# A hybrid layer's single-core kernel: slack in a planned order, rotation tables made once, splits and squares moved between engines

## The chip, the core and the metric

One core of one Trainium2 chip runs the whole layer. The metric is the device time of one execution in microseconds. The five engines are PE (TensorE, matmuls), DVE (VectorE), ACT (ScalarE), POOL (GpSimd) and SP (SyncE, which issues most transfers).

## What is computed

A decoder layer for 2048 tokens of width 1024. One projection feeds latent attention (4 heads), a gated delta rule (4 heads, chunked) and attention over 256 memory tokens; the three are gated, projected and added to x. The reference, cut to what matters:

```python
h = rms_norm(x, norm_in[l])
c_q, c_kv, k_rope, gdn_qkv, gdn_a, gdn_b, mem_q, gate = split_cols(h @ w_in[l], IN_SPLITS)
q = (rms_norm(c_q, q_a_norm[l]) @ w_q_b[l])          # 4 heads of 128 + 64
q_rope = apply_rope(q_rope, cos, sin); k_rope = apply_rope(k_rope, cos, sin)
kv = (rms_norm(c_kv, kv_a_norm[l]) @ w_kv_b[l])
o_mla = causal_mla(q_nope, q_rope, k_nope, k_rope, v_mla)
qkv = silu(causal_depthwise_conv(gdn_qkv, gdn_conv[l]))
gq, gk = l2_normalize(gq), l2_normalize(gk)
o_gdn = rms_norm(gated_delta_rule_chunked(gq, gk, gv, g, beta), gdn_norm[l])
o_mem = memory_attention(mem_q, mk, mv)              # mk, mv from rms_norm(mem) @ w_mem_kv
mixed = concatenate([o_mla, o_gdn, o_mem]) * silu(gate)
x = rms_norm(x + mixed @ w_out[l], norm_final)
```

The delta rule solves a triangular system for each chunk and then runs over the chunks in order: `v_new = u - w @ state`, an output from the state and `v_new`, and `state = state * decay + k.T @ v_new`. The reference's chunk is 64 tokens; the kernel takes steps of 128.

## The kernel before

**Tiles and stages.** The sequence is worked in two halves of 1024 tokens, each in two blocks of 512. Matrices lie with features in the 128 partitions. A product in full precision is made of three fast ones: both sides are split into a high part and a rest (`hh`, `hl` of the normed input; `wh`, `wl` of a weight tile `wr`; `bwh`, `bwl` of a weight tile `bw`), so a group of projection matmuls in the trace reads hh,wh / hl,wh / hh,wl. The high part is a cast on ACT, the rest a subtraction on DVE or GpSimd. Matmul results of the projection are named `ip`.

**The opening.** x is loaded transposed; `prepare` splits it for a block and sums its squares into `acc` over eight tiles (squares on ACT, adds on GpSimd or DVE). `channel_rms` reduces that to the inverse norm of each token (tiles xss, nt, rc), `dg` is a diagonal matrix of it, and PE spreads it over the partitions (`rb`), from where ACT copies it to `rms`. `abt` is the first result scaled by it.

**The delta rule.** For every half and head, `delta_head` is a coroutine. It takes the norms of q and k (`sums`, `norms`, `nt`), loads rows that scale them (`fr`) and a decay row (`gr`) for each block, builds `kq` and its products `kk`, lets GpSimd solve the 32x32 diagonal blocks in 62 small operations (`pr`, `X`; input `lt`, output `tsys`), doubles the inverse on PE (`inv`, `mid`) and then runs eight scan steps. A step is: PE `pa` from the state; DVE `r`; PE; ACT `vn`; PE; DVE the new state (`st` and `st_odd` in turn); PE the output. The small tables of decays are the tiles `tks` and, turned by PE through `pc`, `cols`. Convolution blocks (`conv`) write `raw`, whose first three columns are the history `hist` of the block before, and make `y` of it.

**What sets the order.** Nobody writes the order out. A planner in the kernel's Python code keeps a clock for each engine (`T`), adds a modelled cost to it for every instruction, and walks through the projection units; after every three matmuls `pump` looks through the coroutines in the background. A coroutine that says `yield d` is resumed when the planner's PE clock has passed the modelled end of its last step (`step_end`) by d nanoseconds. So a `yield` sets how much other PE work comes between two dependent steps. Every engine then runs its own instructions in exactly that order, and waits where an operand is not there. `lesser` gives the subtraction of a split to GpSimd when GpSimd's clock, and a time called `solving`, are no later than PE's clock plus some slack, and else to DVE. `dma` puts a transfer on SP's queue in the order of its modelled times.

**Rotation tables.** `trig_tables` makes sine and cosine of all positions in two passes of 1024 positions, on 128 partitions in which the 32 frequencies stand four times; products on GpSimd, sines on ACT; the result goes to memory. `key_rope` and the rotation of q load `cs` and `sn` from there.

## Time and profile before

| | us |
|---|---|
| median of 3 runs (1838.02 to 1842.04) | 1840.38 |
| the profiled execution's own time | 1840.0 |
| its span in the trace | 1838.2 |
| PE busy | 1745.6 (95%) |
| DVE busy | 1200.7 (65%) |
| ACT busy | 737.7 (40%) |
| GpSimd busy | 546.9 (30%) |

The mean granted clock of PE is 0.98. The shares are averages over stages: the opening to about 60 us, projections with convolutions to about 170, projections beside solves and scans to about 1000, the hand-over to attention to about 1200, attention and the output projection to the end. A wait in brackets in a timeline is the idle time ahead of an instruction and what ended it.

### The profile page before, as it was taken

How to read it: one execution, taken by the hardware profiler on the slowest of the kernel's cores; microseconds unless marked ns; L12 is line 12 of the kernel's file. 1: busy time of each engine (PE TensorE's matmuls, PEld its weight loads, DVE VectorE, ACT ScalarE, POOL GpSimd, SP SyncE). 2: the span in 40 equal slices, each digit the busy share in tenths (PEclk: the TensorE clock that was granted, in tenths of full speed). 3: DMA queues.
4: the chain of work that ended last, by engine and by line, in shares of the span. 5: the costliest groups of instructions: out<-in, count | busy, mean ns of one | idle time of the engine just before them, and what ended most of it. 6: DMA issues, size and time to landing. Idle time of an engine off the chain costs nothing. (4 is left out here: it accounts for less than half of the span.)

```text
span 1838.2 us, 28677 instructions
## 1 busy us (share of the span) xinstructions
PE 1745.6 (95%) x9780; PEld 1466.7 (80%) x9780; DVE 1200.7 (65%) x2710; ACT 737.7 (40%) x1798; POOL 546.9 (30%) x918
## 2 busy tenths in 40 slices
PE   6898999999989999999998799999999999999998
PEld 5676778787777788888887687889999989878886
DVE  8878796567776777646667363677776778345443
ACT  6354243234343445324444322455555556322121
POOL 6534716341251224443112635001111002412120
PEclk8899999899999999999999999999999999999999
DMA  5444457434646544564566368435252526566551
GB/s 199 154 135 152 149 179 213 132 97 153 199 127 236 166 149 127 176 213 137 171 202 185 99 195 268 139 107 184 67 175 79 155 90 214 165 190 198 176 160 53
DMA packets 226355, 292.51 MB, mean 159 GB/s; under 512 B 30464, under 2 KB 130816, under 8 KB 226208
## 3 DMA queue, kind: packets, MB, share of 16 engines
q1 hardware_dynamic: 219168, 274.94, 47.7%
q0 software_dynamic: 7040, 15.74, 3.0%
q8 instruction: 77, 1.26, 0.3%
q14 instruction: 70, 0.57, 0.1%
HBM read 197.53 MB, written 93.06 MB: 158 GB/s over the span
## 5 line engine op out<-in xcount | busy, mean ns | idle before, releaser
L258 PE MATMUL ip<-hh,wh 128*128 128x512 f32 x1088 | 459.8, 423 | 22.9 <-ACT hh L258 8.4
L258 PE MATMUL ip<-hh,wl 128*128 128x512 f32 x1088 | 434.7, 400 | 5.6 <-DVE wl L258 3.0
L258 PE MATMUL ip<-hl,wh 128*128 128x512 f32 x1088 | 432.4, 397 | 0.2
L258 PEld LDWEIGHTS ip<-hh,wh 128*128 128x128 f32 x1088 | 209.2, 192 | 58.9 <-ACT hh L258 8.4
L258 PEld LDWEIGHTS ip<-hh,wl 128*128 128x128 f32 x1088 | 208.2, 191 | 51.8 <-DVE wl L258 3.8
L258 PEld LDWEIGHTS ip<-hl,wh 128*128 128x128 f32 x1088 | 209.3, 192 | 35.3 <-DVE hl L258 1.1
L258 POOL TENSOR_TENSOR wl<-wr,wh 128x512 fp32r<-128x512 f32 x72 | 98.5, 1368 | 397.5 <-ACT wh L258 374.9
L258 ACT CAST wh<-wr 128x512 fp32r<-128x512 f32 x146 | 90.2, 618 | 144.5 <-PE ip L258 103.8
L258 DVE TENSOR_TENSOR tl<-pt,th 128x512 fp32r<-128x512 f32 (+2 forms) x208 | 119.8, 585 | 28.3 <-ACT th L258 25.9
L258 PE MATMUL sc<-kn,qn 128*128 128x512 f32 (+2 forms) x480 | 134.6, 381 | 0.0
L258 PE MATMUL av<-th,vn 128*128 128x256 f32 x576 | 131.5, 288 | 0.8 <-ACT th L258 0.8
L258 PE MATMUL op<-wop,mh 128*128 128x512 f32 x416 | 130.5, 394 | 0.0
L258 DVE SCALAR_TENSOR_TENSOR y<-raw,gdn_conv,y 128x512 f32<-128x512 f32 x144 | 121.9, 854 | 7.6 <-ACT y L258 6.6
L258 ACT CAST th<-pt 128x512 fp32r<-128x512 f32 (+2 forms) x163 | 82.4, 513 | 102.6 <-PE pt L258 94.1
L258 POOL TENSOR_TENSOR pr<-X,lt 128x60 f32<-128x60 f32 (+24 forms) x248 | 97.8, 394 | 55.7 <-DMA lt<-lsys 37.0
L293 POOL DMA_DIRECT2D mix<-mo x64 | 34.7, 543 | 238.6 <-ACT mo L258 162.2
L258 PEld LDWEIGHTS av<-th,vn 128*128 128x128 f32 x576 | 98.8, 189 | 6.2 <-ACT th L258 2.6
L258 POOL TENSOR_TENSOR X<-X,pr 128x60 f32<-128x60 f32 (+24 forms) x248 | 95.9, 387 | 19.3
L258 PE MATMUL sc<-kr,qr 128*128 128x512 f32 (+2 forms) x320 | 96.7, 381 | 0.0
L258 POOL TENSOR_TENSOR og<-og,orow 128x512 f32<-128x512 f32 x28 | 41.1, 1490 | 170.7 <-DMA orow<-ri 142.9
L258 PEld LDWEIGHTS op<-wop,mh 128*128 128x128 f32 x416 | 77.4, 188 | 17.3
L258 ACT ACTIVATE s<-s,m 128x768 f32<-128x768 f32 (+13 forms) x71 | 79.0, 1114 | 29.8 <-DVE mx L258 29.8
(286 smaller groups left out, 3658.9 us busy)
## 6 DMA issues: line engine op xcount, KB each, us to landing
wr<-in_w_in SPq DMA_DIRECT2D x148, 256.0 KB, 3.4
fr<-rows_n SPq DMA_DIRECT2D x48, 256.0 KB, 3.9
mxo<-mix SPq DMA_DIRECT2D x16, 768.0 KB, 6.0
craw<-craw SPq DMA_DIRECT2D x40, 256.0 KB, 3.1
x<-in_xT SPq DMA_DIRECT2D x32, 256.0 KB, 5.3
gatem<-gt SPq DMA_DIRECT2D x32, 256.0 KB, 2.7
qn<-qn SPq DMA_DIRECT2D x32, 256.0 KB, 2.7
kn<-kn SPq DMA_DIRECT2D x32, 256.0 KB, 3.3
```

Source lines behind the costliest of these rows:

```text
L258: return pinned(f(*args, **kw))
L293: pinned(nc.gpsimd.dma_start(out=raw(out), in_=raw(in_)))
```

## The change

- The scan's steps (`r`, `vn`, the new state) and three other places in `delta_head` wait 700 ns (`SPARE`) of planned PE time beyond the end of the step before; behind some loads (first rows of a head, `el`, rotation tables, decay tables) 1000 to 2000 ns more.
- After a solve, GpSimd is held to be `solving` for 12,000 ns, where it was 5,000.
- The rotation tables are made in one pass of 128x512: four quarters of the positions in the partitions. Their loads repeat a 32x512 table 2 or 4 times.
- Block 0's squares are added on DVE alone; block 1's norm is taken on ACT from rows of x, which are loaded beside the transposed x, and block 1's splits stand behind block 0's norm.
- The two copies between `raw` and `hist` go from DVE to ACT.

```diff
+SPARE = 700.0
-    trig = dt("trig", [2, P, S])
+    trig = dt("trig", [2, 4, 32, 512])
     def trig_tables():
...
-        for b in range(2):
-            bs = slice(b * HALF, (b + 1) * HALF)
-            yield from take(page=3)
-            ang, kk, tmp = (page("trig") for _ in range(3))
+        yield from take(page=2)
+        pg, pt = page("trig"), page("trig")
+        ang, kk, tmp = pg[:, 0:512], pg[:, 512:1024], pt[:, 0:512]
+        pi = kk.bitcast(I32)
+        for c in range(4):
+            dma(out=pi[c * 32:(c + 1) * 32], in_=a["positions"][:, c * 512:(c + 1) * 512].partition_broadcast(32))
...
+    def trig_load(t, i, c, n):
+
+        dma(out=t[0:n * 32],
+            in_=trig[i, c].unsqueeze(0).broadcast_to([n, 32, 512]))
     def key_rope(hf, b):
...
-        dma(out=cs, in_=trig[0, :, c0:c0 + 512])
-        dma(out=sn, in_=trig[1, :, c0:c0 + 512])
-        yield 0
+        trig_load(cs, 0, hf * 2 + b, 2)
+        trig_load(sn, 1, hf * 2 + b, 2)
+        yield 2000
...
         dma(out=bt, in_=ab[hf, 4:8].rearrange("h (c t) -> (h c) t", t=P))
-        yield 2500
+        yield 3500
...
         dma(out=el, in_=rows_l[hf].partition_broadcast(P))
-        yield 0
+        yield 2000
...
-            V.tensor_copy(raw[:, 0:3], hist[:, i, :])
-            V.tensor_copy(hist[:, i, :], raw[:, 512:515])
+            A.copy(raw[:, 0:3], hist[:, i, :])
+            A.copy(hist[:, i, :], raw[:, 512:515])
...
         V.tensor_tensor(kfac, cols[:, 2:4, hs], nk.unsqueeze(1).broadcast_to([P, 2, 8]), op=ALU.mult)
-        yield 0
+        yield SPARE
...
         kq = page("kq").rearrange("p (c i t) -> p c i t", c=4, i=2)
-        yield 0
+        yield 2000
...
             if b == 0:
                 cur = rows(1)
+                yield SPARE
...
-        solving[0] = T["POOL"] + 5000
+        solving[0] = T["POOL"] + 12000
...
             V.scalar_tensor_tensor(r, pa[:, 0:P], kfac[:, 0, c:c + 1], vt[:, c % 4, :],
                                    op0=ALU.mult, op1=ALU.add)
-            yield 0
+            yield SPARE
...
             A.copy(vn, pa[:, 128:256])
-            yield 0
+            yield SPARE
...
             step_end[0] = t
-            yield 0
+            yield SPARE
...
             V.tensor_tensor(ob3, ob3, inv_ro[:, b * 4:b * 4 + 4].unsqueeze(2).broadcast_to([P, 4, P]), op=ALU.mult)
-            yield 0
+            yield SPARE
...
-                dma(out=cs, in_=trig[0, :, c0:c0 + 512])
-                dma(out=sn, in_=trig[1, :, c0:c0 + 512])
-                yield 0
+                trig_load(cs, 0, hf * 2 + b, 4)
+                trig_load(sn, 1, hf * 2 + b, 4)
+                yield 2000
...
-        accs = [t2("acc") for _ in range(2)]
+        acc = t2("acc")
...
-            (G if T["POOL"] <= T["DVE"] + 600 else V).tensor_tensor(accs[b], accs[b], sq, op=ALU.add)
+            V.tensor_tensor(acc, acc, sq, op=ALU.add)
...
+        grab(page=4)
+        rows = [page("xrow") for _ in range(4)]
+        for j, t in enumerate(rows):
+            dma(out=t, in_=a["x"][(4 + j) * P:(5 + j) * P, :], first=True)
...
-        for k in range(KT // 2):
-            prepare(1, k, xs1[k])
         def behind(b):
-            step_end[0] = ready(accs[b])
-            yield 0
-            parts = yield from channel_rms(accs[b], D)
+            if b == 0:
+                step_end[0] = ready(acc)
+                yield 0
+                parts = yield from channel_rms(acc, D)
+            else:
+                parts = inverse_rms((yield from token_sums(rows, 4)), D)
+                give(page=4)
...
             if b == 0:
-                for k in (4, 5):
-                    prepare(1, k, xs1[k])
+                for k in range(4):
+                    x_split(1, k, xs1[k])
             yield EARLY
             yield from row
             if b == 0:
-                for k in (6, 7):
-                    prepare(1, k, xs1[k])
+                for k in range(4, KT):
+                    x_split(1, k, xs1[k])
```

How it moves instructions, at three places. First DVE in the opening, from the first split of x on (wp is a weight tile of the first unit, tks a decay table). Before:

```order
L258 SCALAR_TENSOR_TENSOR hl<-x,norm_in,hh 128x512
L258 TENSOR_TENSOR wl<-wp,wh 128x512 x3
L258 SCALAR_TENSOR_TENSOR hl<-x,norm_in,hh 128x512 x4
L258 TENSOR_TENSOR wl<-wp,wh 128x512 x3
L258 MEMSET tks 32x128
L258 TENSOR_TENSOR wl<-wp,wh 128x512
L258 SCALAR_TENSOR_TENSOR hl<-x,norm_in,hh 128x512 x7
L258 TENSOR_REDUCE xss<-sq 128x4
```

and now:

```order
L259 SCALAR_TENSOR_TENSOR hl<-x,norm_in,hh 128x512
L259 TENSOR_TENSOR wl<-wp,wh 128x512 x3
L259 SCALAR_TENSOR_TENSOR hl<-x,norm_in,hh 128x512
L259 TENSOR_TENSOR acc<-acc,sq 128x512
L259 SCALAR_TENSOR_TENSOR hl<-x,norm_in,hh 128x512
L259 TENSOR_TENSOR acc<-acc,sq 128x512
L259 SCALAR_TENSOR_TENSOR hl<-x,norm_in,hh 128x512
L259 TENSOR_TENSOR acc<-acc,sq 128x512
L259 SCALAR_TENSOR_TENSOR hl<-x,norm_in,hh 128x512
L259 TENSOR_TENSOR acc<-acc,sq 128x512
L259 TENSOR_TENSOR wl<-wp,wh 128x512 x4
```

The sums of squares stand between the splits of x on DVE, and four `hl` fewer stand ahead of the norm's reduction.

Second PE in the first head's scan, from the step that reads the state st_253 (inv_279 and inv_280 are the inverse's buffers). Before:

```order
L258 MATMUL pa<-st_253,y 128x128
L258 MATMUL pa<-vn,aT 128x128
L258 MATMUL pa<-st_odd,y 128x128
L258 MATMUL inv<-inv_280,mid 64x64 x7
L258 MATMUL pa<-r,inv_279 128x128
L258 MATMUL inv<-inv_280,mid 64x64
L258 MATMUL ip<-hh,wh 128x512
L258 MATMUL ip<-hl,wh 128x512
L258 MATMUL ip<-hh,wl 128x512
L258 MATMUL pa<-vn,kt 128x128
L258 MATMUL kk<-kq,y 128x256 x2
L258 MATMUL pa<-st_odd,y 128x128
```

and now:

```order
L259 MATMUL pa<-st_253,y 128x128
L259 MATMUL pa<-vn,aT 128x128
L259 MATMUL ip<-hh,wh 128x512
L259 MATMUL ip<-hl,wh 128x512
L259 MATMUL ip<-hh,wl 128x512
L259 MATMUL ip<-hh,wh 128x512
L259 MATMUL ip<-hl,wh 128x512
L259 MATMUL ip<-hh,wl 128x512
L259 MATMUL pa<-st_odd,y 128x128
L259 MATMUL ip<-hh,wh 128x512
L259 MATMUL ip<-hl,wh 128x512
L259 MATMUL ip<-hh,wl 128x512
```

Between the step from st_253 and the one from st_odd stood the output of the step alone; now two projection groups stand there, and groups stand behind it too.

Third GpSimd behind the third solve of the second half, from the solve's stores on (cmask is the causal mask, lsys_3_104 the fourth system). Before:

```order
L293 DMA tsys_2_111<-X 256x1x32 x4
L293 DMA inv_279<-tsys_2_111 32x8x32 x4
L293 DMA X<-in_eye 128x256
L258 TENSOR_TENSOR bwl<-bw,bwh 128x512 x4
L258 TENSOR_TENSOR wl<-wr,wh 128x512
L258 MEMSET mid 32x8x32
L258 TENSOR_TENSOR bwl<-bw,bwh 128x512 x3
L258 TENSOR_TENSOR wl<-wr,wh 128x512
L258 TENSOR_TENSOR bwl<-bw,bwh 128x512 x2
L258 MEMSET cmask 128x512
L1328 AFFINE_SELECT cmask<-cmask 128x512
L258 TENSOR_TENSOR wl<-wr,wh 128x512
```

and now:

```order
L294 DMA tsys_2_111<-X 256x1x32 x4
L294 DMA inv_279<-tsys_2_111 32x8x32 x4
L294 DMA X<-in_eye 128x256
L259 TENSOR_TENSOR wl<-wr,wh 128x512
L259 MEMSET cmask 128x512
L1334 AFFINE_SELECT cmask<-cmask 128x512
L259 MEMSET mid 32x8x32
L259 TENSOR_TENSOR wl<-wr,wh 128x512 x2
L294 DMA lt<-lsys_3_104 32x1024 x4
```

All nine `bwl` are gone from GpSimd here; a weight split `wl` stays behind the stores.

The second place again, on PE near the end of the scans in the second half, in the changed order alone (kt, y and aT are operands of the scan):

```order
L259 MATMUL pa<-r,inv_279 128x128
L259 MATMUL pa<-vn,kt 128x128
L259 MATMUL pa<-st_255,y 128x128
L259 MATMUL pa<-vn,aT 128x128
L259 MATMUL pa<-st_odd,y 128x128
L259 MATMUL pa<-r,inv_279 128x128
L259 MATMUL pa<-vn,kt 128x128
L259 MATMUL pa<-st_odd,y 128x128
L259 MATMUL pa<-vn,aT 128x128
L259 MATMUL pa<-st_255,y 128x128
L259 MATMUL ip<-hh,wh 128x512
L259 MATMUL ip<-hl,wh 128x512
```

Ten matmuls of the scan stand here with no other work between them.

## Rows read from the trace of the kernel before

**Rows 1.** Windows, two stages: start:end, length, busy us of each engine, PE clock, DMA.

```profile
170.00:1000.00 830.00, 792.34 (x4317) 650.07 (x4316) 566.53 (x1198) 318.41 (x822) 285.01 (x529) 0.98 0.54 168
1000.00:1200.00 200.00, 187.51 (x1206) 159.78 (x1205) 106.65 (x270) 75.74 (x210) 80.03 (x174) 0.96 0.57 171
```

**Rows 2.** PE's waits, whole run: waited for, us in total, times, longest.

```profile
PE pa L258 <- DVE st_odd L258: 10.0, 7, 4.5
...
PE ip L258 <- DVE elo L258: 7.7, 1, 7.7
PE pc L258 <- DVE tks L258: 7.4, 3, 4.5
...
PE pa L258 <- DVE r L258: 5.5, 3, 3.2
PE oT L258 <- DVE nt L258: 5.0, 1, 5.0
PE pa L258 <- DVE st L258: 4.1, 4, 1.7
PE kk L258 <- DVE kq L258: 3.9, 2, 2.1
```

**Rows 3.** Windows, two stretches with a granted clock of 0.50.

```profile
326.10:336.30 10.20, 8.66 (x37) 7.33 (x38) 5.91 (x13) 1.16 (x3) 0.00 (x0) 0.50 0.05 16
1053.10:1059.90 6.80, 3.20 (x12) 2.92 (x13) 4.97 (x6) 3.43 (x7) 4.02 (x4) 0.50 0.70 223
```

**Rows 4.** Timeline of PE, opening: start, us, instruction, count, [idle before, releaser].

```profile
32.90 0.39 PE L258 MATMUL ip<-hh,wl 128*128 128x512 f32 x1
37.53 1.39 PE L258 MATMUL rb<-dg,ones 128*128 128x512 f32 x2 [4.23 <-DVE dg L258]
42.01 0.76 PE L258 MATMUL ip<-hh,wh 128*128 128x512 f32 x1 [3.09 <-DVE abt L258]
```

**Rows 5.** Groups on DVE by shape, 11 to 32 us: busy us, mean ns, idle before.

```profile
L258 DVE SCALAR_TENSOR_TENSOR hl<-x,norm_in,hh 128x512 fp32r<-128x512 f32 x11 | 14.9, 1406 | 0.4 <-ACT hh L258 0.4
```

**Rows 6.** Timeline of DVE, behind the opening's norm.

```profile
39.25 0.74 DVE L258 SCALAR_TENSOR_TENSOR hl<-x,norm_in,hh 128x512 fp32r<-128x512 f32 x1
```

**Rows 7.** Groups on GpSimd by shape, 11 to 45 us.

```profile
L258 POOL TENSOR_TENSOR acc<-acc,sq 128x512 f32<-128x512 f32 x14 | 21.7, 1549 | 11.4 <-ACT sq L258 10.7
```

**Rows 8.** Timeline of DVE, first pass of the rotation tables.

```profile
78.88 2.17 DVE L258 TENSOR_TENSOR nt<-nt,xss 128x4 f32<-128x4 f32 x1
```

**Rows 9.** Instructions of tile trig on GpSimd: ns minimum/median/maximum, first and last start.

```profile
L258 POOL TENSOR_TENSOR trig<-trig x8: 2338/2391/2837, 78.7 to 152.1; 128x1024 f32<-128x1024 f32 x8
```

**Rows 10.** Timeline of PE, second pass of the rotation tables.

```profile
148.40 0.66 PE L258 MATMUL ip<-hh,wl 128*128 128x512 f32 x1 [2.96 <-DVE wl L258]
```

**Rows 11.** Timeline of PE, first head's scan.

```profile
327.64 0.80 PE L258 MATMUL pa<-st,y 128*128 128x128 f32 x2 [4.50 <-DVE st_odd L258]
...
328.65 0.64 PE L258 MATMUL pa<-st_odd,y 128*128 128x128 f32 x2
```

**Rows 12.** Timeline of DVE, the same place.

```profile
325.43 0.69 DVE L258 TENSOR_TENSOR gr<-gr,cols 128x512 f32<-128x512 f32 x1 [5.87 <-DMA gr<-rows_g]
...
329.32 0.35 DVE L258 SCALAR_TENSOR_TENSOR r<-pa,kfac,vt 128x128 f32<-128x128 f32 x1 [0.29 <-PE pa L258]
```

**Rows 13.** Waits of SP's DMA queue, 1030 to 1062 us.

```profile
SPq L304 <- POOL bwl L258: 13.6, 2, 11.6
```

**Rows 14.** Timeline of DVE, hand-over to attention.

```profile
1052.15 0.69 DVE L258 TENSOR_TENSOR gr<-gr,cols 128x512 f32<-128x512 f32 x1 [12.77 <-DMA gr<-rows_g]
```

**Rows 15.** Groups on DVE by shape, whole run: the copies into raw.

```profile
L258 DVE COPY raw<-hist 128x3 f32<-128x3 f32 x48 | 15.0, 312 | 0.4
```

**Rows 16.** ACT's waits, whole run.

```profile
ACT wh L258 <- PE ip L258: 103.8, 59, 6.0
...
ACT raw L258 <- DVE y L258: 50.0, 25, 10.6
```

**Rows 17.** Queues of the page: packets, MB, share of 16 engines' time.

```profile
q1 hardware_dynamic: 219168, 274.94, 47.7%
```

More of the change, by code (lines that the diff above doesn't have):

```diff
@@ L498, in trig_tables @@
         magic = 1.5 * 2.0**23
-        for b in range(2):
-            bs = slice(b * HALF, (b + 1) * HALF)
-            yield from take(page=3)
-            ang, kk, tmp = (page("trig") for _ in range(3))
-            pi = kk.bitcast(I32)
-            dma(out=pi, in_=a["positions"][:, bs].partition_broadcast(P))
-            yield 0
-            V.tensor_copy(ang, pi)
-            yield 0
-            G.tensor_tensor(ang, ang, invf.broadcast_to([P, HALF]), op=ALU.mult)
-            G.tensor_scalar(kk, ang, 1.0 / (2 * math.pi), magic, op0=ALU.mult, op1=ALU.add)
-            G.tensor_scalar(kk, kk, 1.0, -magic, op0=ALU.mult, op1=ALU.add)
-            yield 0
-            for c in parts:
-                G.tensor_scalar(tmp, kk, -c, 0.0, op0=ALU.mult, op1=ALU.add)
-                G.tensor_tensor(ang, ang, tmp, op=ALU.add)
-                yield 0
-            V.tensor_scalar(ang, ang, -3.1415925, 3.1415925, op0=ALU.max, op1=ALU.min)
-            yield 0
-            A.activation(kk, ang, AF.Sin)
-            A.activation(ang, ang, AF.Abs)
-            A.activation(ang, ang, AF.Sin, bias=halfpi, scale=-1.0)
-            yield 0
-            dma(out=trig[1, :, bs], in_=kk)
-            dma(out=trig[0, :, bs], in_=ang)
-            yield 0
-            give(page=3)
@@ new lines, in trig_tables @@
+        yield from take(page=2)
[5 more added lines that the diff above has]
+        yield 0
+        V.tensor_copy(ang, pi)
+        yield 0
+        G.tensor_tensor(ang, ang, invf.broadcast_to([P, 512]), op=ALU.mult)
+        G.tensor_scalar(kk, ang, 1.0 / (2 * math.pi), magic, op0=ALU.mult, op1=ALU.add)
@@ new lines, in trig_tables @@
+        G.tensor_scalar(kk, kk, 1.0, -magic, op0=ALU.mult, op1=ALU.add)
+        yield 0
+        for c in parts:
+            G.tensor_scalar(tmp, kk, -c, 0.0, op0=ALU.mult, op1=ALU.add)
+            G.tensor_tensor(ang, ang, tmp, op=ALU.add)
+            yield 0
+        V.tensor_scalar(ang, ang, -3.1415925, 3.1415925, op0=ALU.max, op1=ALU.min)
+        yield 0
+        A.activation(kk, ang, AF.Sin)
+        A.activation(ang, ang, AF.Abs)
+        A.activation(ang, ang, AF.Sin, bias=halfpi, scale=-1.0)
@@ L526, in trig_tables @@
+        yield 0
+        for i, t in ((1, kk), (0, ang)):
+            dma(out=trig[i].rearrange("c f t -> (c f) t"), in_=t)
+        yield 0
+        give(page=2)
         done["trig"] = True
+    def trig_load(t, i, c, n):
+        dma(out=t[0:n * 32],
+            in_=trig[i, c].unsqueeze(0).broadcast_to([n, 32, 512]))
     def evac_split(ps, dst, n=512):
@@ L718, in key_rope @@
     def key_rope(hf, b):
-        c0 = hf * HALF + b * 512
         while "trig" not in done:
@@ L1035, in delta_head @@
                                    op0=ALU.mult, op1=ALU.add)
-            yield 0
+            yield SPARE
             vn = sb.tile([P, P], F32, name="vn", tag="vn", bufs=2)
@@ L1039, in delta_head @@
             A.copy(vn, pa[:, 128:256])
-            yield 0
+            yield SPARE
             PE.matmul(pa[:, 256:384], kt[:, c % 4, :], vn, start=True, stop=True)
@@ L1047, in delta_head @@
             step_end[0] = t
-            yield 0
+            yield SPARE
         give(scan=1, P2=1, TT=1, page=1)
@@ L1070, in delta_head @@
             V.tensor_tensor(ob3, ob3, inv_ro[:, b * 4:b * 4 + 4].unsqueeze(2).broadcast_to([P, 4, P]), op=ALU.mult)
-            yield 0
+            yield SPARE
             ps = psg("oT")
@@ L1939, in split, with prepare @@
             return wh, wl
-        accs = [t2("acc") for _ in range(2)]
-        def prepare(b, k, x):
-            x_split(b, k, x)
+        acc = t2("acc")
+        def prepare(k, x):
+            x_split(0, k, x)
             if k == 0:
-                A.activation(accs[b], x, AF.Square)
+                A.activation(acc, x, AF.Square)
                 return
@@ L1956, in x_opening @@
             if i == 0:
-                prepare(0, 0, xs[0])
+                prepare(0, xs[0])
         for k in range(1, KT):
-            prepare(0, k, xs[k])
+            prepare(k, xs[k])
             xs1.append(x_load(1, k - 1))
@@ L1966, in x_opening @@
                 dma(out=t, in_=src, awaited=False)
-        for k in range(KT // 2):
-            prepare(1, k, xs1[k])
         def behind(b):
-            step_end[0] = ready(accs[b])
-            yield 0
-            parts = yield from channel_rms(accs[b], D)
+            if b == 0:
+                step_end[0] = ready(acc)
+                yield 0
+                parts = yield from channel_rms(acc, D)
+            else:
+                parts = inverse_rms((yield from token_sums(rows, 4)), D)
+                give(page=4)
             row = rms_row(b, parts)
```

2 lines of the change are left out of this document (removed).

## The prediction

> **What bounds the kernel now.** I read the stages first, the waits of TensorE (PE) second, and then each place where a large wait ends. The stage table [rows 1] shows PE busy for 792.34 of 830 us in the long middle, where projections, GpSimd solves and the delta rule's scan run beside each other, and for 187.51 of 200 us where they hand over to attention. VectorE (DVE) is busy for 566.53 of the same 830 us, GpSimd (POOL) for 285.01. So PE is the bound, its instructions hardly change in number (four transposes fewer), and the change can only give back time in which PE waits or runs at the lower clock. The list of PE's waits [rows 2] says what it waits for: the delta rule's own steps on DVE (st_odd 10.0, r 5.5, st 4.1 us), one wait of 7.7 for elo, 7.4 for the decay rows' chain tks, 5.0 for the norm nt, 3.9 for kq. After a long wait PE runs slow for some us: granted clock 0.50 of 2.4 GHz, which is its 1.2 GHz level, in both stretches of [rows 3], each of which begins inside a wait. What that costs is half of the busy time in it: 8.66 / 2 = 4.3 us after 326.1, and 3.20 / 2 = 1.6 us after 1053.1.
>
> The profiled execution took 1840.0 us by its own clock, span 1838.2, and the median of the runs is 1840.38. They are so near that I subtract from 1840 and correct nothing.
>
> **Opening: squares off GpSimd.** PE ends block 0's first 96 projections at 33.3, waits 4.23 us for dg, runs two matmuls and waits 3.09 us more for abt [rows 4]. In front of dg stands DVE, late: its eleven hl operations between 11 and 32 us take 1406 ns each [rows 5], one that runs when GpSimd is quiet takes 0.74 us [rows 6]. What runs beside them is GpSimd's sum of squares, 14 adds of 1549 ns [rows 7]. The change takes all of them off GpSimd: seven go to DVE, the seven of block 1 vanish (its norm is summed on ACT from rows of x). For DVE: 11 x (1.41 - 0.74) = 7.4 us saved, 7 adds at about the 0.74 us of [rows 6] = 5.2 added, and four hl operations of block 1 behind the norm instead of ahead of it, 4 x 0.74 = 3.0 less. The reduction then starts some 5 us earlier, dg is there at about 31, and the first wait goes. The second wait stays, since PE reaches the rb matmuls at about 33.5 and ACT now has two long squares of the row tiles in front of its copy. From rb to the next projection it took 42.01 - 37.53 = 4.5 us before; I take 4 to 5 of that again, so PE resumes at 37.5 to 38 instead of 42.0. Four to 4.5 us, and the deferred hl cover less of the half clock behind it: **5 us**, bounds 2 and 8.
>
> The Trainium skill ("SBUF — State Buffer", section "Who interferes with whom") calls the port pair that DVE and GpSimd share an exclusive lock, whose loser blocks for a whole instruction. The trace agrees in [rows 8]: a 128x4 operation took 2.17 us beside GpSimd's products of 2391 ns [rows 9]. By that rule the seven added DVE adds cost GpSimd nothing here, as it has no more work in the opening, so the sum is unchanged.
>
> **Rotation tables once.** Before, they are made in two passes of 128x1024 tiles. Their eight GpSimd products take 2391 ns each [rows 9] and DVE's small operations stall beside them [rows 8]. The second pass, at 128 to 155 us, is gone: the one that is left works on 128x512, all four quarters in the partitions. Beside the second pass PE waited 2.96 us for a weight split [rows 10] and, in two waits, 3.9 us for kq [rows 2]. I count 2.96 + 3.9 = 6.9 and take **6 us** of it, as other work moves into the place; bounds 0 and 9. The 7.4 us for tks in the first pass I leave: its chain is shorter by the stalls of [rows 8], but PE also reaches it earlier, by the opening's 5 us and by the order, where less work stands ahead. Zero, bounds -4 and +5.
>
> **Slack on the delta rule's steps.** A coroutine is resumed when the planner's PE clock has passed the end of its last step; 700 ns is now added after r, vn and the new state. The order shows its effect: st_253 and st_odd stood two matmuls apart and now six projections stand between. Before, the three kinds of step waits cost 10.0 + 5.5 + 4.1 = 19.6 us [rows 2], and the half clock behind the largest 4.3 [rows 3]: 23.9. The largest, 4.50 us [rows 11], isn't of the steps' making: DVE sat until 325.43 for a row load gr, 5.87 us, with st_odd queued behind it [rows 12]. That load is a second block's, which gets no slack of its own; it goes only if the new order parts the two, as I think it does, since there the first head's scan runs among the convolutions. I take 0.7 of 23.9: **17 us**, bounds 0 and 24. The norm's oT wait of 5.0 us [rows 2] gets the same 700 ns, which by itself covers little; I take **3**, bounds 0 and 5.
>
> **No splits on GpSimd while it solves.** `solving` now holds it out for 12 us after a solve, not 5. At 1030 to 1062 SP's queue stood 11.6 us for a buffer that GpSimd's bwl had to release [rows 13], behind the solve's last transfers. Everything queued on SP behind it came late: DVE waited 12.77 us for a gr load [rows 14], with elo queued behind, and PE 7.7 for elo [rows 2]. The order has nine of these splits gone from GpSimd there, and DVE, which waits at that place, takes them. Gain 7.7 + 1.6 of clock [rows 3] = **9 us**, bounds 0 and 12.
>
> **What it costs.** The slack needs other PE work, and near the end of the scan there is none. In the changed order some ten matmuls of pa stand in a row before the last projections. One handover, PE to DVE and back, is 328.65 to 329.67, about 1.0 us [rows 11, 12]; eight of them without filler are **-8 us**, bounds -15 and 0 (attention could move in front of them). The history copies, 48 + 48 of 128x3, move from DVE (312 ns [rows 15], at most 96 x 0.312 = 30 us) to ACT, which is busy for 318.41 of the middle's 830 us [rows 1]; zero, with the rival below for when they are not hidden. Four more loads of x rows on SP in the opening stand behind x's own: nothing.
>
> Sum: 5 + 6 + 17 + 3 + 9 - 8 = 32; with about 3 us for small waits and clock dips between (bounds 0 and 6): **1840 - 35 = 1805 us.**
>
> **Rivals.** *The waits are dealt anew.* Every yield shifts the whole order. The gr wait of [rows 12] shows that steps stall on what is queued before them on DVE, not on their own length, and such meetings arise elsewhere. Then the steps give nothing, the rest 5 + 6 + 9 - 8 = 12: 1828. For it: the second block's loads have no slack. Against: it needs new collisions as costly as those taken away.
>
> *Slower: ACT is held by the copies.* ACT works in order. In the first half `raw` is written by DVE, so the copy of its history must wait for DVE, and the wh cast and vn copy behind it wait too. ACT already waits 50.0 us, 25 times, longest 10.6, for DVE's y [rows 16], so DVE lags that far at times. Against: wh casts wait 103.8 us for PE to free a buffer [rows 16], so they run ahead. It decides from the point where ACT stands longer than a split's lead of 24 matmuls, at the middle's mean of 792.34 / 4317 = 0.18 us [rows 1] some 4.4 us. At 24 blocks x 2.5 us = 60, half to all paid: 1835 to 1865, I say 1850.
>
> *Table loads on few engines.* The cosine and sine tiles are now loaded as 2 or 4 copies of a 32x512 table, with the copies outermost. If each copy goes to one DMA engine, an engine moves 64 KB. The main queue moved 274.94 MB in 47.7% of 16 engines' time [rows 17], which is 274.94 / (0.477 x 16 x 1838.2) = 19.6 KB per us, so 3.3 us for one table and 6.7 for the pair, against 1.7 over all engines. Eight pairs x 5 us late, of which the 2 us of new slack behind each covers some: 24 to 40 us, 1829 to 1845. I say 1837. For it speaks the Trainium skill ("DMA: Bandwidth & Descriptors", section "Rules for kernel authors"): an outermost dimension under 16 confines the transfer to as many engines. No run here shows such a load yet. Against its price: q rotation is far from PE's next need, and other loads wait only on those engines.
>
> *More is freed:* all bounds near their good ends, and small waits with them: 1778.
>
> **How the numbers follow.** Chances: forecast 0.54 (1788 to 1818), dealt anew 0.20 (1818 to 1838), ACT held 0.12, few engines 0.06, more freed 0.08. A measurement of this kernel can tell about 0.2% from no change, 3.7 us: 1836.7 to 1844. Faster: 0.54 + 0.16 + 0.08 + 0.03 = 0.81; within: 0.04 + 0.02 = 0.06; slower: 0.12 + 0.01 = 0.13. The range leaves out the slower cases and the last tenth of the good ones: 1772 to 1836.
>
> **What would show it.** Right: in the profile after, PE's first projection of block 1 starts before 38.5; no GpSimd operation named acc, and no trig after 110 us; PE's waits for st_odd, r and st sum to under 8 us; no SP wait of over 6 us for bwl around the scan's end; a gap of about 8 us between pa matmuls just before the last projections. Wrong: waits of pa as large as before at other places (dealt anew); waits `raw` or `wh` on ACT for DVE with PE behind them (ACT held); cs and sn loads landing after 8 us or more (few engines).

## The result and the profile after

The changed kernel takes 1819.3 us (median of 4 runs, 1815.38 to 1822.34) against 1839.2 before in the same comparison: a ratio of 0.9893, 95% interval 0.9864 to 0.9921, so a gain of 14 to 25 us. The forecast was 1805 us, a gain of 35, in a range of 1772 to 1836. The sign and the range held; the size did not, and one term of the sum has the wrong sign. The profiled execution after is the slowest of its four, 1822.34 us by its own clock.

The stages after, where [rows 1] has two of them (start and end, length, busy us of each engine with its instructions, granted PE clock, DMA share, GB/s):

```profile
0.00:60.00 60.00, 47.16 (x187) 37.12 (x188) 42.51 (x93) 37.28 (x68) 11.21 (x16) 0.97 0.75 248
60.00:170.00 110.00, 102.97 (x446) 82.94 (x445) 87.17 (x182) 48.36 (x133) 33.98 (x24) 0.95 0.45 133
170.00:1000.00 830.00, 802.06 (x4374) 661.15 (x4373) 538.92 (x1092) 317.26 (x868) 287.49 (x529) 0.99 0.52 166
1000.00:1200.00 200.00, 184.89 (x1207) 158.94 (x1206) 118.50 (x300) 77.94 (x226) 70.50 (x174) 0.94 0.58 169
```

In the 830 us of the middle PE is busy for 802.06 where it was 792.34. At the hand-over to attention it is busy for 184.89 of 200 us where it was 187.51, at a clock of 0.94 where it was 0.96: that stage got worse. The waits of PE, to be read beside [rows 2] (total, times, longest):

```profile
PE inv L259 <- DVE mid L259: 6.6, 3, 5.3
PE pt L259 <- DVE vt L259: 6.0, 1, 6.0
PE pa L259 <- DVE st L259: 5.8, 6, 2.0
...
PE pa L259 <- DVE st_odd L259: 4.9, 4, 2.4
...
PE pa L259 <- DVE r L259: 2.6, 3, 1.7
PE pa L259 <- ACT vn L259: 2.6, 5, 1.3
...
PE pc L259 <- DVE tks L259: 2.4, 2, 2.3
```

The scan's step waits (st, st_odd, r, vn) sum to 15.9 us. Before, the three of [rows 2] came to 19.6, with vn's 0.7 to 20.3. Elo fell from 7.7 to 1.1 us and tks from 7.4 to 2.4; mid rose from 2.8 to 6.6, and 6.0 in attention (pt) are new.

**Where the time went.** To compare two orders of the same work, I gave each kind of matmul a standard step (start to next start, the third decile over all traces of this study), summed the steps along PE's row, and read at which time each kernel had done so much work. The excess is that time less the work (us):

| work done | 40 | 160 | 440 | 680 | 920 | 1040 | 1600 |
|---|---|---|---|---|---|---|---|
| excess before | 22.7 | 47.9 | 101.0 | 118.2 | 158.7 | 176.6 | 192.8 |
| excess after | 18.4 | 32.4 | 57.3 | 100.3 | 116.8 | 158.6 | 175.9 |
| excess after, slack set to 0 (x_spare0, below) | 15.8 | 30.4 | 58.9 | 94.1 | 125.0 | 139.1 | 153.1 |

At 440 us of work the change is 43.7 us ahead. Between 440 and 680 it gives back 26, between 680 and 920 it wins 24 more, and between 920 and 1040, at the hand-over, it gives back 24 again. So the forecast's 35 us were there, and more, in the first part of the kernel, and more than half was lost in the second. At 1600 us of work the last two rows are 22.8 us apart, as are the two profiled executions (1822.34 and 1799.71). By the ratios below it is 12: the profiled execution after is its slowest, and the kernel before took 1839.2 us there against 1833.6 beside x_spare0.

**The opening** (answers to [rows 4], [rows 5] and [rows 7]). On PE the first rb, which waits no more, and the first projection of block 1; on DVE the splits of x and the sums of squares:

```profile
34.11 0.61 PE L259 MATMUL rb<-dg,ones 128*128 128x512 f32 x2
37.27 0.47 PE L259 MATMUL ip<-hh,wh 128*128 128x512 f32 x1 [2.55 <-DVE abt L259]
```

```profile
L259 DVE SCALAR_TENSOR_TENSOR hl<-x,norm_in,hh 128x512 fp32r<-128x512 f32 x8 | 6.0, 750 | 7.0 <-ACT hh L259 7.0
L259 DVE TENSOR_TENSOR acc<-acc,sq 128x512 f32<-128x512 f32 x7 | 4.8, 688 | 0.0
```

The hl operations fell from 1406 to 750 ns, and a sum of squares takes 688 ns on DVE where it took 1549 on GpSimd. PE resumes at 37.27 instead of 42.01.

**A load behind a split behind a solve.** This is the largest wait between 440 and 680 us of work. First SP's queue, then GpSimd, DVE and PE in order of cause:

```profile
SPq L305 <- POOL wl L259: 7.3, 1, 7.3
```

```profile
749.51 2.32 POOL L294 DMA_DIRECT2D inv<-tsys  x4 [5.41 <-DMA tsys<-X]
...
752.43 1.31 POOL L259 TENSOR_TENSOR wl<-wr,wh 128x512 fp32r<-128x512 f32 x1
```

```profile
759.62 0.69 DVE L259 TENSOR_TENSOR gr<-gr,cols 128x512 f32<-128x512 f32 x1 [8.60 <-DMA aT<-at]
...
761.55 0.89 DVE L259 STREAM_TRANSPOSE mid<-inv 32x256 f32<-32x256 f32 x2
```

```profile
762.12 1.44 PE L259 MATMUL inv<-mid,LT 32*32 32x32 f32 x32 [5.28 <-DVE mid L259]
```

GpSimd issued a solve's last transfers at 749.51, came to a weight split only at 752.43, SP stood 7.3 us for the buffer that this split had to release, the decay row gr behind it arrived so late that DVE stood 8.60 us, and the transposes of mid behind gr kept PE for 5.28 us. (The row of 759.62 names aT, a load that SP issued after gr and that can't be what this operation reads; the order of the issues points to gr.) It is the chain of [rows 13] and [rows 14] at another place: with 12 us of hold it is gone at 1045 us and appears at 752.

**At the hand-over**, DVE and PE:

```profile
1127.18 0.69 DVE L259 TENSOR_SCALAR_CACHE_REDUCE s<-sc 128x512 f32<-128x512 f32 x1 [5.99 <-POOL pr L259]
```

```profile
1130.84 1.73 PE L259 MATMUL pt<-ident,s 128*128 128x128 f32 x7 [6.04 <-DVE vt L259]
```

A tile s of attention takes over memory that the last solve still reads (s and the solve's input lt are buffers of one pool in the code). DVE stands until the solve's last pr, 5.99 us, with all of attention's reductions behind it, and PE 6.04.

### The profile page after: what moved, and what is told of

Its sections match the earlier page's. It is cut to its first block, busy times and chain, and to the rows that moved or that the text cites. A ratio compares the mean times of both kernels' runs of the same rounds, so it can differ in the third digit from the quotient of the medians.

```text
span 1820.6 us, 28632 instructions
## 1 busy us (share of the span) xinstructions
PE 1746.9 (96%) x9776; PEld 1471.2 (81%) x9776; DVE 1158.6 (64%) x2622; ACT 734.6 (40%) x1884; POOL 500.4 (27%) x894
## 4 chain that ended last, share of the span: by engine, by line
PE 54%; DMA 4%; DVE 3%; POOL 1%; issue 1%; ACT 1%; SPq 1%; DVEq 0%; ACTq 0%; POOLq 0%
PE op L259 14%; PE ip L259 13%; PE sc L259 9%; PE av L259 7%; PE pt L259 4%; PE pa L259 2%; PE qb L259 1%; PE inv L259 1%; DVE y L259 1%; PE kk L259 1%; DMA craw<-craw 1%; SPq L305 1%; PE kb L259 1%; PE mk L259 1%; POOL X L259 1%
## 5 line engine op out<-in xcount | busy, mean ns | idle before, releaser
L259 POOL TENSOR_TENSOR wl<-wr,wh 128x512 fp32r<-128x512 f32 x84 | 120.2, 1431 | 493.9 <-ACT wh L259 403.9
L259 DVE SCALAR_TENSOR_TENSOR y<-raw,gdn_conv,y 128x512 f32<-128x512 f32 x144 | 116.5, 814 | 16.1 <-ACT y L259 14.7
L259 POOL TENSOR_TENSOR pr<-X,lt 128x60 f32<-128x60 f32 (+24 forms) x248 | 92.4, 373 | 49.2 <-DMA lt<-lsys 30.3
L259 PE MATMUL pt<-ident,s 128*128 128x128 f32 x544 | 84.2, 276 | 6.2 <-DVE vt L259 6.0
```

Of the source, the lines that this page charges most:

```text
L259: return pinned(f(*args, **kw))
```

## The experiments

All ratios are against the kernel before, timed on the same chip in the same comparison; the kernel before had medians of 1833.6 to 1835.1 us there.

### The slack taken out, and put in alone

x_spare0 is the changed kernel with

```diff
-SPARE = 700.0
+SPARE = 0.0
```

> The changed kernel with the slack of 700 ns set to 0 at all its places. Theory 'the slack pays' (the forecast's term of 17 + 3 - 8 us): 1819 + 12 = 1831, and PE's waits for st_odd, st, r and vn rise from 15.9 us in sum to over 22. Rival 'the slack gives nothing': the gain of the change comes from its other parts, and the planned gaps before attention (3.7 us of waits and 3.4 of half clock at 1092 to 1103 us) go: 1812 to 1819, waits of the steps within 4 us of 15.9.

b_spare is the kernel before with the slack alone, at its six places (the expectation says seven, a miscount):

```diff
+SPARE = 700.0
...
-        yield 0
+        yield SPARE
```

> The kernel before with the slack of 700 ns alone, at the seven places. Theory 'the slack pays': 1839 - 12 = 1827, PE's waits for st_odd, st, r and vn fall from 20.3 us to under 10. Rival 'the slack gives nothing': 1836 to 1842, with those waits at other places, since most of them were DVE queued behind a load, as at 325.43 us.

Without the slack the changed kernel takes **1800.26 us**, ratio 0.9827 (0.9801 to 0.9853). The slack alone makes the kernel before slower: **1867.25 us**, ratio 1.0191 (1.0156 to 1.0226). Both theories fell: the slack neither pays nor gives nothing. It costs 12 us in the one order (0.9893 - 0.9827 = 0.0066 of 1835, give or take 7 by the two intervals) and 35 in the other (0.0191). The step waits of x_spare0 are

```profile
PE pa L259 <- DVE st L259: 3.8, 4, 2.2
...
PE pa L259 <- DVE st_odd L259: 3.2, 4, 1.1
PE pa L259 <- DVE r L259: 3.1, 3, 1.9
```

and 1.3 for vn, 11.4 us in sum, against 15.9 with the slack: in the changed order it does not even shorten them. In the kernel before they fell from 20.3 to 15.2, so 5 us were there to be had by it.

One place where it costs is the end of b_spare's last scan, on PE:

```profile
1217.45 0.49 PE L259 MATMUL pa<-r,inv 128*128 128x128 f32 x2 [0.44 <-DVE r L259]
1218.30 0.49 PE L259 MATMUL pa<-vn,kt 128*128 128x128 f32 x2 [0.35 <-ACT vn L259]
1219.22 0.49 PE L259 MATMUL pa<-st,y 128*128 128x128 f32 x2 [0.44 <-DVE st_odd L259]
1219.55 0.39 PE L259 MATMUL pa<-vn,aT 128*128 128x128 f32 x2
1219.77 0.39 PE L259 MATMUL pa<-st_odd,y 128*128 128x128 f32 x2
```

The parts of the step follow each other with nothing between, and each handover waits 0.35 to 0.44 us. The same stretch, from the last projection to the last scan step, in three kernels, x_spare0, after and b_spare (columns as in the stages above):

```profile
1113.00:1170.90 57.90, 57.75 (x460) 51.12 (x459) 42.67 (x148) 29.08 (x83) 4.36 (x12) 1.00 0.45 142
```

```profile
1110.50:1208.80 98.30, 88.22 (x645) 78.20 (x643) 61.60 (x195) 42.91 (x130) 24.42 (x73) 0.93 0.44 126
```

```profile
1136.50:1232.70 96.20, 80.39 (x531) 66.21 (x530) 51.22 (x176) 33.64 (x106) 27.79 (x85) 0.87 0.53 157
```

Without the slack PE is busy for 57.75 of 57.90 us at full clock. With it the stretch is 98.3 us long with 10 us idle at a clock of 0.93, and in b_spare 96.2 with 16 idle at 0.87.

### Why: the row of heads becomes late

Heads are worked one after the other: solve, inverse, scan. The scan's eight steps carry three slacks of 0.7 us each, 16.8 us for a head. The last solve ends at 1127.4 us with the slack and at 1097.0 without, 30.4 later, about two heads' worth; in the kernel before it moved from 1134.4 to 1181.1, 46.7, about three. That these delays are the slack summed along the row fits in size and is not shown step by step. When the projections have run out first, there is too little to put between. For all kernels of this study: when the last solve ends against the start of the last projection, and what the stretch from 920 to 1040 us of work adds to the excess:

| kernel | last solve against last projection, us | excess added, us |
|---|---|---|
| y_spread3 | -17 | 16.3 |
| y_late15 | -17 | 14.2 |
| x_spare0 | -16 | 14.1 |
| y_dvecopy | -16 | 13.8 |
| before | -16 | 17.9 |
| y_solv5 | -16 | 19.1 |
| b_open | -13 | 25.6 |
| y_load0 | -11 | 15.5 |
| s_half1 | +2 | 36.5 |
| s_half2 | +7 | 42.6 |
| after | +17 | 41.8 |
| x_spread | +18 | 42.0 |
| b_spare | +45 | 55.9 |
| x_solve | +60 | 61.8 |

The second column follows the first: 14 to 26 us where the solve is done before the last projection, 36 to 62 where it isn't. That part of the excess is bare steps, as above, a lower clock (0.93 and 0.87 in the two stretches above), and engines that work in order and stand for the late solve's result with attention behind them. For the last of these, x_solve's DVE:

```profile
1169.43 1.69 DVE L259 STREAM_TRANSPOSE mid<-inv 32x256 f32<-32x256 f32 x4 [11.18 <-DMA inv<-tsys]
```

DVE stands 11.18 us for the transfer of the inverse, and PE 11.10 for what DVE makes of it. All six kernels in which the solve is late have one such stand of DVE at the hand-over, for the last solve's final `pr` or its inverse: 6.0 us in after, 7.5 in x_spread, 8.3 in s_half1, 9.8 in b_spare, 11.2 in x_solve and 11.5 in s_half2. In the other eight no wait of this kind at the hand-over, from 1000 us on, exceeds 4.7 us.

s_half2 and s_half1 set the slack in one half's heads alone, at all six places:

```diff
-            yield SPARE
+            yield SPARE * (hf == 1)
```

> The changed kernel with the 700 ns of slack in the second half's heads alone. Theory 'late chain': the slack draws out the row of heads (solve, inverse, scan, one after the other), and in the second half there are at last no projections to fill it. With the slack the last solve ended at 1127.4 us, without it at 1097.0, and in the kernel before with the slack added at 1181.1 instead of 1134.4. Then the cost sits in the second half: 1815 to 1825, last solve's end over 1115 us, and over 20 us of excess of PE between the last projections and the last scan step. Rival 'slack costs everywhere' (each step's slack adds planned idle wherever it stands): about half of the 19 us, 1808 to 1812. Rival 'lottery of orders': any value between 1800 and 1835, with no link to the end of the last solve.

(and `hf == 0` in s_half1)

> The changed kernel with the slack in the first half's heads alone. Theory 'late chain': the first half has projections of the second behind it to fill the gaps, so nothing is lost there, and the forecast's gain on the steps may show: 1795 to 1803, last solve's end within 8 us of 1097. Rival 'slack costs everywhere': 1808 to 1812. Rival 'lottery of orders': any value between 1800 and 1835.

In the second half alone: **1824.35 us**, ratio 0.9948 (0.9930 to 0.9967), with the solve late by 7 us, as expected. That is 22 us more than without slack, where the whole slack costs 12. In the first half alone: **1812.22 us**, ratio 0.9893 (0.9862 to 0.9925). That is not the harmless thing it was to be: the last solve ended at 1110.0, 13 us later than without slack and outside the 8 us expected. Its excess before the hand-over, at 920 us of work, is 113.7 against 125.0 without slack, so the first half did gain some 11 us up to there, and then lost 22 more at the hand-over (36.5 against 14.1). No slack stands in the second half here, so the 22 us are not gaps of its own steps. DVE and PE at the hand-over show what they are in part:

```profile
1118.95 0.43 DVE L259 STREAM_TRANSPOSE mid<-inv 32x256 f32<-32x256 f32 x1 [8.31 <-DMA inv<-tsys]
```

```profile
1121.02 0.79 PE L259 MATMUL pa<-st_odd,y 128*128 128x128 f32 x2 [8.46 <-DVE st L259]
```

DVE stood 8.31 us for the last solve's inverse, with a scan step's new state and attention queued behind, and PE 8.46 for that state. So a lateness made in the first half also arrives at the end. The costs of the two halves, 22 and 12 us, do not add up to the whole slack's 12; how much of each is this lateness and how much the new deal of the order is open.

A delay by itself, y_late15, put into x_spare0:

```diff
         solving[0] = T["POOL"] + 25000
-        yield 2000
+        yield 2000 + (15000 if hf == 1 and h == 3 else 0)
```

> The changed kernel without the slack, with one delay: the last head of the second half resumes its solve 15 us of planned PE time later. All of the order up to the last eighth of the projections stays as it was. Theory 'late chain': in ten profiles the excess of PE's time over its work at the hand-over grows with how much later the last solve ends than the last projection starts (-16 us: 16 to 20 us of excess; +2: 38; +8 to +19: 43 to 44; +45 and +60: 58 and 64). Without the slack it is -16 and 16. With the delay it should be about 0, the excess 30 to 38, and the time 1800 + 14 to 22 = 1814 to 1822. Rival 'the slack's own gaps' (each step's 0.7 us costs where it stands): no slack stands here, so 1798 to 1804.

**1802.56 us**, ratio 0.9825 (0.9810 to 0.9839): no change. But the edit did not do what it was to do. GpSimd had nothing else between, so the solve ended at 1095.8 us as before (1097.0); only the last scan step moved, from 1170.9 to 1182.2. It shows that a scan that ends 11 us later costs nothing as long as the solve is in time. So no lever of its own moved the solve alone. For a late solve as the cause stand the order of the table, the stand of DVE in all six late kernels, and s_half1, which has that stand without slack in the second half. Against treating it as the whole cause: all six late kernels have slack somewhere, and the stand is 6 to 11.5 us where the excess is 22 to 48 us above x_spare0's.

### The other parts

**The hold on GpSimd**, y_solv5: x_spare0 with the old value.

```diff
-        solving[0] = T["POOL"] + 12000
+        solving[0] = T["POOL"] + 5000
```

> The changed kernel without the slack, and with GpSimd held for 5 us behind a solve as before instead of 12. Theory 'the hold pays' (the forecast's term of 9 us): 1800 + 9 = 1809, with bwl splits on GpSimd behind the last solves, an SP wait for them of over 6 us and a DVE wait for gr of over 8. Rival 'the hold gives nothing here': 1797 to 1803.

**1832.37 us**, ratio 0.9995 (0.9980 to 1.0011), against 0.9827 with the hold: 31 us where 9 were forecast. SP's waits for GpSimd, whole run, first with 5 us (y_solv5), then with 12 (x_spare0):

```profile
SPq L305 <- POOL wl L259: 208.3, 56, 19.3
...
SPq L305 <- POOL bwl L259: 30.1, 7, 14.5
```

```profile
SPq L305 <- POOL wl L259: 140.9, 52, 7.7
...
SPq L305 <- POOL bwl L259: 6.5, 4, 1.9
```

238 us with a longest of 19.3, against 147 with a longest of 7.7. DVE's waits for gr are 26.2 and 14.8 us. The forecast priced one such chain, at 1045 us; the excess from 160 to 920 us of work is 121 in y_solv5 and 95 in x_spare0, so the price lies along the whole middle. But this is one order against another. The kernel before, also with 5 us, has 157 us of these waits and 111 us of that excess, so much of y_solv5's loss is not the 5 us by themselves. And y_solv5, which has the changed opening, the tables made once, the moved copies and the slack behind loads, ends at the time of the kernel before: the parts of this change don't add, and the 31 us are no price of the hold alone.

**The solve's planned time**, x_solve: the planner reckons 15.7 us for a solve; in the traces before and after the sixteen solves take 22.8 to 33.7 us.

```diff
         if op == "tensor_tensor":
-            return 147 + 2.1 * free(out)
+            return 250 + 4 * free(out) if free(out) < 100 else 147 + 2.1 * free(out)
```

> The changed kernel with one number altered: the planner's cost of the small GpSimd operations of a solve is 250 + 4 ns per element, where it was 147 + 2.1. By the old cost a solve takes 15.7 us; in the two traces the sixteen solves take 22.8 to 33.7 us. Theory 'solve underestimated': GpSimd is planned free some 10 us before it is, so that a weight split stood behind a solve's transfers at 752 us (SP's queue waited 7.3 us for it, the gr load behind it was late, PE waited 5.28 us at 762.12), and attention's s took over a buffer that the fourth solve still read (DVE waited 5.99 us at 1127.18, PE 6.04 us at 1130.84). With the true cost both go, with 3.4 and 5 us of half clock: about 1819 - 5.3 - 6.0 - 5 = 1803. Rival 'waits dealt anew': a new order brings other meetings of the same size: 1814 to 1824, with new PE waits of 3 us and more.

**1853.06 us**, ratio 1.0120 (1.0085 to 1.0155). Both expectations missed. With the truer cost the last solve ends 60 us behind the last projection, the farthest of all, and the hand-over costs 61.8 us. The likely reason, not shown, is that the planner now puts all that follows a solve later. An honest cost made the order worse here, where the row of heads was already the late part.

**The opening alone**, b_open: the kernel before with the changed block of the opening (its part of the diff ahead of the prediction, nothing else).

> The kernel before with the opening's part alone: block 0's squares added on DVE, block 1's norm on ACT from rows of x, block 1's splits behind the norm. The forecast's term is 5 us: the first projection of block 1 at 37 to 38 us instead of 42.01, and the fortieth us of PE work reached 4 to 6 us earlier. The whole time, if the rest of the order stayed: 1834 to 1836. If the gain at the fortieth us is there and the whole differs by more than 5 us from that, the order behind it decides, and single parts can't be priced by whole times.

**1846.59 us**, ratio 1.0068 (1.0046 to 1.0090), slower, while at 40 us of work it is 4.7 us ahead (58.0 against 62.7), as forecast. What came after was dealt anew: by 160 us of work the lead is gone, and among its PE waits are one of 10.5 us for elo and one of 6.5 for r. So the part is worth its 5 us in place, and its whole time says nothing on it.

**The tables' loads.** In the changed kernel DVE, the DMA engines and PE at the first rotation of q:

```profile
562.55 0.69 DVE L259 TENSOR_TENSOR ra<-qb,cs 128x512 f32<-128x512 f32 x1 [6.57 <-DMA cs<-trig]
565.55 0.69 DVE L259 TENSOR_TENSOR rb<-qb,sn 128x512 f32<-128x512 f32 x1 [2.31 <-DMA sn<-trig]
...
566.76 0.34 DVE L259 SCALAR_TENSOR_TENSOR st_odd<-st,el,pa 128x128 f32<-128x128 f32 x1
```

```profile
562.00:566.00 4.00, 2.76 (x14) 1.95 (x12) 1.14 (x2) 0.00 (x0) 0.00 (x0) 1.00 0.31 106
```

```profile
567.15 0.80 PE L259 MATMUL pa<-st,y 128*128 128x128 f32 x2 [2.39 <-DVE st_odd L259]
```

cs was issued at 555.54 and was there 7 us later, sn took 9.4, and at 562 to 566 us a share of 0.31 of the DMA engines was busy, 5 of 16. (At 550 to 556 us all were busy, share 1.00, so part of the 7 us can be the queue ahead.) The Trainium skill ("DMA: Bandwidth & Descriptors", section "Rules for kernel authors") says that an outermost dimension under 16 confines a transfer to as many engines; the trace agrees. x_spread stores each table four times and loads plain tiles:

```diff
-            dma(out=trig[i].rearrange("c f t -> (c f) t"), in_=t)
+            for r in range(4):
+                dma(out=trig[i, :, r], in_=t)
...
-            in_=trig[i, c].unsqueeze(0).broadcast_to([n, 32, 512]))
+            in_=trig[i, c, 0:n].rearrange("r f t -> (r f) t"))
```

> The changed kernel with one thing altered: the rotation tables are stored four times, so that a load of cs or sn is a plain tile whose partitions are outermost, not 2 or 4 copies of a 32x512 table. Theory 'few engines': in the changed kernel's trace cs was issued at 555.54 us and DVE waited for it until 562.55 (6.57 us), then 2.31 us for sn, and at 562 to 566 us only 0.31 of the DMA engines were busy, that is 5 of 16. Then the loads land in 4 to 5 us, those waits go, and with them PE's wait of 2.39 us for st_odd at 567.15 and about 1.7 us of half clock: 1815, 4 us less than the changed kernel's 1819.3. Rival 'crowded queue': the DMA engines were all busy (share 1.00) at 550 to 556 us, the loads were late because of what was in front; then they still take 7 to 9 us and the time stays at 1819.

**1834.46 us**, ratio 0.9999 (0.9986 to 1.0011). DVE has no wait for cs or sn left, as the theory had it, but the stores now have an outermost dimension of 4 themselves. SP there, the share of DMA engines that is busy meanwhile (the number before the last), and ACT:

```profile
93.34 11.94 SPq L305 DMA_DIRECT2D trig<-trig  x4
```

```profile
93.30:106.00 12.70, 12.70 (x64) 10.48 (x63) 6.37 (x9) 7.86 (x30) 2.35 (x2) 1.00 0.26 92
```

```profile
116.78 0.62 ACT L259 CAST wh<-wr 128x512 fp32r<-128x512 f32 x1 [13.68 <-DMA wr<-in_w_in]
```

There are eight stores of 256 KB in a row. The first four took 2.9 us to issue, the last four the 11.94 us above, while 0.26 of the engines were busy, 4 of 16. By an estimate from the 19.6 KB per us and engine of [rows 17] (64 KB in 3.3 us), eight such stores take 26 us on four engines; ACT had the weight loaded behind them at 116.78, 26.4 us after the first store's issue at 90.40. That fits the same confinement. ACT stood 13.68 us for that weight and PE 14.7. y_spread3 (without slack) cuts the loads instead:

```diff
-        dma(out=t[0:n * 32],
-            in_=trig[i, c].unsqueeze(0).broadcast_to([n, 32, 512]))
+        for r in range(n):
+            dma(out=t[r * 32:(r + 1) * 32], in_=trig[i, c])
```

> The changed kernel without the slack, with each table load cut into 2 or 4 loads of one 32x512 table, so that 32 partitions are outermost in each. Theory 'few engines': DVE's waits for cs and sn, 9.4 us without the slack and 12.7 with it, fall under 2 us, as they did where the table was stored four times (none there; but there four stores with an outermost of 4 took 11.94 us to issue, and PE lost 14.9 us behind them). PE's waits near 545 to 600 us get 2 to 5 us smaller: 1795 to 1799. Rival: 32 more issues on SP of about 0.45 us each delay what is behind them: 1800 to 1806.

**1802.89 us**, ratio 0.9828 (0.9810 to 0.9847), the same as x_spare0, again with no wait of DVE for cs or sn (9.4 us in x_spare0). So the few engines cost nothing that can be measured here without the slack.

**The slack behind loads**, y_load0, from x_spare0:

```diff
-        yield 3500
+        yield 2500
...
-        yield 2000
+        yield 0
         pc = psg("pc")
...
         kq = page("kq").rearrange("p (c i t) -> p c i t", c=4, i=2)
-        yield 2000
+        yield 0
```

> The changed kernel without the slack and without the 1000 to 2000 ns behind the loads of decay tables, el and a head's first rows. Theory 'late chain': each head's chain is 2 us shorter, the last solve ends earlier still against the last projection, which is no use below -16, so that stage stays within 4 us; the DVE waits for gr, 11.9 us in the changed kernel and 40.8 in the one before, come back to over 30, and some of them reach PE: 1803 to 1812. Rival 'the loads' slack gives nothing': 1797 to 1803.

**1806.43 us**, ratio 0.9855 (0.9839 to 0.9872) against 0.9827: inside the expected range, but by other means. gr's waits for its own row were 8.3 us and one of 9.0 is put down to a weight's load, against 14.8 in x_spare0 and over 30 expected; those of kq for its rows rose from 10.9 to 16.3. Its interval and x_spare0's overlap; the three kernels without slack that ran in the same comparison (0.9811 to 0.9828) are some 5 us faster. So this slack may pay a little, and why is open.

**The copies**, y_dvecopy, from x_spare0:

```diff
-            A.copy(raw[:, 0:3], hist[:, i, :])
-            A.copy(hist[:, i, :], raw[:, 512:515])
+            V.tensor_copy(raw[:, 0:3], hist[:, i, :])
+            V.tensor_copy(hist[:, i, :], raw[:, 512:515])
```

> The changed kernel without the slack, with the 96 copies between raw and hist on DVE as before. The forecast's term is zero: 1797 to 1803. 'DVE is relieved': if the 27 us of copies that left DVE mattered, the steps' waits for DVE rise by 5 us or more and the time to 1805 to 1812. 'ACT held' (the slower rival of the forecast): the copies on ACT cost, and the time falls below 1796.

**1799.68 us**, ratio 0.9811 (0.9797 to 0.9826): no difference on either engine, as forecast.

x_spare0, the change without its slack on the steps, beats both kernels: about 1.7% under the kernel before where the change has 1.1%.

## Why the prediction was right and wrong

- **Opening, 5 us: right, with one step by luck.** hl at 750 ns (0.74 assumed), the seven added sums 4.8 us (5.2), dg begun at 30.94 (31), PE resumed at 37.27 (37.5 to 38). The norm's reduction started 3.9 us earlier and not 5 (28.13 for 32.00), since DVE stood 2.47 us for the sums on PE; from there to dg it took 2.8 us where it had taken 4.8 beside GpSimd's work. The forecast had neither, and they nearly cancel. At 40 us of work 4.3 us ahead in the whole change, 4.7 alone.
- **Tables once, 6 + 0 us: direction right, perhaps too small.** Between 40 and 160 us of work the change gains another 11.2 us; no run has the tables alone, so their part of it is not set apart. The zero taken for tks was the bad part: its wait fell from 7.4 to 2.4, the good end of the bounds given. In the second place, a split's wait of 4.0 us is still there at 137 us, though GpSimd's part of the tables is done by 84.
- **Slack on the steps, 17 + 3 us, and -8 for it: wrong in sign.** Taken out of the whole change it is worth -12 us, not +12. The step that failed is the factor of 0.7 on 23.9 us. The text itself had seen that the largest wait was a load's and not a step's, and still let the slack take most of the sum; the waits of the steps fell by 5 us in b_spare, and in the change by 9 without the slack (20.3 to 11.4) and by 4 with it. In the changed kernel st_odd, r and st sum to 13.3 us, where the forecast named under 8 as a sign of being right. The cost was sized by the ten bare matmuls that the order showed (-8, bounds -15 and 0). What the runs show instead is the last solve 30.4 us later, behind the end of the projections, and 41.8 - 14.1 = 28 us more excess at the hand-over, of which one stand of 6 us is traced to that solve and the rest lies in the lower clock, bare steps and smaller waits.
- **Hold on GpSimd, 9 us: mechanism seen, size open.** The chain priced at 1045 us is gone, and it stands once more at 752. Taking the hold out of x_spare0 costs 31 us, but that mixes the hold with a new order, as said above.
- **Copies, 0: right** (0.9811 and 0.9827). ACT's copies take 190 ns each, and ACT waits 28.7 us in all before them for DVE's raw; y_dvecopy shows no cost of that.
- **The rivals.** 1819.3 lies just inside the band of "dealt anew" (1818 to 1838, chance 0.20) and just outside the forecast's own (1788 to 1818). Its mechanism, new meetings in place of the old, is seen: the 762.12 chain, b_open's +12 us. But it gave the steps nothing, and the slack cost. "Few engines" exists as described, 7 to 9 us to landing against the forecast's 6.7 for the pair, but its price of 24 to 40 us isn't there: one PE wait of 2.39 us, at 567.15. "ACT held" did not come.

So the total lay nearer than its parts, by luck: what the other parts gave together beyond the forecast (0.0173 of 1834 = 32 us, where 5 + 6 + 9 + 3 = 23 were forecast) covered 9 of the 24 us by which the slack's term was off. Open are the share of chance in any single order, and the 43 us of excess between 440 and 680 us of work (17 before, 35 without slack), in which six waits of 1.7 to 5.3 us stand, 16.6 in sum, without a common cause.

## What to carry to other kernels

Before slack is put between dependent steps, add it up along the whole serial chain and ask what work is left to fill it when the chain ends: 0.7 us here is 16.8 per head, and the last solve ended 30.4 us later, with no projections left. A wait of a step is only the step's own if nothing else stood in front of it on the engine it waits for; follow it back before a remedy is priced. And where every edit reorders everything, price a part in its place, at equal work done, not by the whole time.

## What the runs showed of the hardware

- A load or store whose outermost dimension is 4 ran on few DMA engines: a share of 0.31 (loads) and 0.26 (stores) busy, and 7 to 9 us to landing for 256 KB, where an estimate by [rows 17]'s rate over 16 engines gives 0.8. Of eight such stores in a row the first four took 2.9 us to issue and the last four 11.94, with all later loads of that queue behind them.
- GpSimd was slowed beside DVE as DVE was beside GpSimd (hl, 1406 against 750 ns, in the opening): a split of 128x512 that takes 1.31 us on GpSimd (752.43 above) took 4.33 us while DVE worked through a row of operations of about 0.7 us with two or more inputs.

```profile
132.46 4.33 POOL L259 TENSOR_TENSOR wl<-wr,wh 128x512 fp32r<-128x512 f32 x1 [14.05 <-ACT wh L259]
```

The Trainium skill ("SBUF — State Buffer", section "Who interferes with whom") calls the port pair of the two an exclusive lock; the 3 us more are over four DVE operations of 0.7 us, so one wait for one instruction doesn't explain them; whether GpSimd lost several times or was slowed inside the operation is not shown.
